# Unnormalised softmax, two products per value block, and fractional shares of background work in an attention stage on one Trainium2 core

## The chip, the cores and the metric

The kernel runs on one core of one Trainium2 chip. The core has a matrix engine (PE, with a weight-load track PEld), a vector engine (DVE), an activation engine (ACT), a general engine (POOL, GpSimd) and a queue engine (SP) that mostly starts DMAs. The engines run their own instruction streams in order and wait for each other through semaphores. The metric is the device time of one execution in microseconds; lower is better. All times below are microseconds unless marked ns.

## The reference, cut to what matters

One layer of a streaming encoder: a half-step feed-forward block, one combined projection, sparse attention beside a convolution module, a gated merge with an output projection, and a second half-step feed-forward block. There are 1088 rows (1024 prompt rows and 64 sample rows). The part that the change touches:

```python
z = u @ w_in                       # [q | k | v | q_idx | k_idx | w_idx | conv in | branch gates]
# attention: 8 heads of 64 in 2 groups; each query keeps its top-k admissible keys
logits = einsum('bqcgd,bqncd->bqcgn', qg, kg) * HEAD_DIM ** -0.5
p = softmax(where(valid, logits, -inf))
o = einsum('bqcgn,bqncd->bqcgd', p, vg)
# convolution module
conv_out = silu(layernorm(dc)) @ conv_w_out
# merge
g_a, g_c = split(sigmoid(gate + b_gate), 2)
merged = g_a * (attn @ attn_w_out) + g_c * conv_out
h = h + merged @ w_out
```

All arithmetic is in 32 bits. A product with full precision is made of three matrix products of reduced operands: each operand is split into a high and a low part, and high x high, high x low and low x high are added up in PSUM (`mm3`).

## The kernel before

Activations lie with channels on partitions and rows in the free dimension. Rows are cut into three chunks of 364, 362 and 362 columns (`CHUNKS`). The stages in order: first feed-forward block, combined projection with convolution and indexer, search for the top-k thresholds on DVE, attention, output projection, second feed-forward block. Weights come in by DMA on SP (`wload`: `raw`), are split by ACT (`whi`) and POOL (`wlo`), and the buffers are three deep.

**The gates.** `gates` computes the 16 gate tiles, each three steps (one for each chunk) of 24 matmuls, and ACT's tanh and a DMA (started on ACT's queue) that writes them to DRAM (`d_g`). The first `GPRE` = 8 tiles run ahead of attention, while DVE is still busy with the search; the others are background work of the attention stage.

**Attention.** Queries are taken in nine tiles (`ATILES`): eight of 128 rows with 128 (i + 1) keys, and tile 8 with 64 rows and 192 keys. The order is `TORD` = 8, 5, 6, 7, 4, 3, 2, 1, 0. Each tile has four pairs of heads. For a pair, `soft` computes the logits (two matmuls `lg` for each head and half, L999 and L1000), DVE adds the mask and takes the maximum (L1002), then small DVE instructions join the halves and scale (L1008, L1010), ACT takes the exponential with its sum (L1012), DVE the reciprocal (L1014), and POOL (first head) and DVE (second head) multiply the weights `pr` by it (L1016). `turn` takes a slot of up to two key blocks, transposes four pieces of `pr` by PE (`pt`, L1026) and splits them by ACT and DVE (`ph`, `pl`). `values` adds up the values with `mm3`, so three matmuls of 256 columns for a block with a stationary operand 64 columns wide (`vt`: high or low part); the result `pv` has 64 partitions. After the last block ACT copies it (`oh`) and a DMA writes it to DRAM (`d_at`).

Logits run `AHEAD` = 2 pairs ahead, values `LAG` = 2 slots behind.

**Background work.** `fill` is called once for each slot (84 slots in all) and runs so many steps of `background` as `FILL` has for the tile. Background is one chain: the remaining gates; `norm` of chunk 2 (layer norm of the convolution's output, read from `d_dc`); `conv_out` of chunks 2, 1, 0, each with the `norm` of the chunk that follows; `merge` of chunk 2, which loads the attention's output (`ar`), splits it (`ah`, `al`) and, for each of eight output tiles, loads a gate (`ga`) and a convolution tile (`mpt`), makes 12 matmuls and combines them on DVE (L1162, L1163); `wout` of chunk 2; `merge` of chunk 1. A `merge` starts only after `ready` has found the attention tiles of its chunk done. After attention come `wout` of chunk 1, `merge` of chunk 0, `wout` of chunk 0.

**PSUM.** There are eight banks. Before attention, four belong to `ps4` (used by the gates) and four to `lgi` (indexer, DVE part of the convolution, search). At the start of attention these are closed and pools are opened in this order: `lgp` (three banks, logits), `psf` (two, background), `psa` (two, transposes), `pvp` (one, values). The order of the instructions on each engine is made when the program is built, from the order in which the code issues them, priorities, and a model of when each could run.

## Time and profile before

| what | us |
|---|---|
| median of three runs | 2391.95 (2390.51 to 2393.91) |
| the profiled execution | 2394.14 |
| its span, first to last instruction | 2392.3 |
| PE busy in the span | 2300.3 |
| DVE, POOL, ACT busy in the span | 1658.8, 1407.1, 1146.8 |
| attention stage, from the first logits to the last values | 1157.5 to 1536 |

Times inside the span count from its first instruction. PE is nearly always marked busy. Matmuls overlap, so the duration of one (289 ns for 272 columns) is more than its share of PE's time; what one costs in a full stream is the distance from its start to the next one's start.

### The profile page before, as it was taken

How to read it: one execution, taken by the hardware profiler on the slowest of the kernel's cores; microseconds unless marked ns; L12 is line 12 of the kernel's file. 1: busy time of each engine (PE TensorE's matmuls, PEld its weight loads, DVE VectorE, ACT ScalarE, POOL GpSimd, SP SyncE). 2: the span in 40 equal slices, each digit the busy share in tenths (PEclk: the TensorE clock that was granted, in tenths of full speed). 3: DMA queues.
4: the chain of work that ended last, by engine and by line, in shares of the span. 5: the costliest groups of instructions: out<-in, count | busy, mean ns of one | idle time of the engine just before them, and what ended most of it. 6: DMA issues, size and time to landing. Idle time of an engine off the chain costs nothing.

```text
span 2392.3 us, 43870 instructions
## 1 busy us (share of the span) xinstructions
PE 2300.3 (96%) x16762; PEld 2272.8 (95%) x16762; DVE 1658.8 (69%) x3606; ACT 1146.8 (48%) x2189; POOL 1407.1 (59%) x861
## 2 busy tenths in 40 slices
PE   5999999999999999999899899899999999999997
PEld 5999999999999999999898889899999999999997
DVE  7666678677567387579535897468766678776676
ACT  5433445444335546875644565345433445334343
POOL 4555556555556686889853455457455565445554
PEclk9999999999999999999999999999999999999999
DMA  4232332332223443333322446753232332332223
GB/s 166 89 104 91 98 98 90 125 107 98 89 90 121 143 138 121 91 120 120 106 78 96 125 135 204 254 167 113 80 100 92 107 103 72 108 108 97 89 98 117
DMA packets 130116, 271.90 MB, mean 114 GB/s; under 512 B 18032, under 2 KB 77296, under 8 KB 129904
## 3 DMA queue, kind: packets, MB, share of 16 engines
q1 hardware_dynamic: 114688, 253.48, 32.6%
q10 hardware_dynamic: 15216, 15.60, 2.0%
q8 instruction: 132, 2.16, 0.4%
q14 instruction: 80, 0.66, 0.1%
HBM read 230.34 MB, written 38.75 MB: 112 GB/s over the span
## 4 chain that ended last, share of the span: by engine, by line
PE 76%; DVE 9%; DMA 6%; POOL 4%; issue 2%; ACT 2%; SPq 0%; ACTq 0%; DVEq 0%; POOLq 0%
PE ps L154 24%; PE ps L156 24%; PE ps L155 24%; POOL ac L695 3%; DMA ga<-d_g 1%; PE pt L1026 1%; PE lgi L806 1%; PE lgi L807 1%; DMA d_h<-hr 1%; DVE ga L1163 1%; DMA raw<-wf 1%; DMA raw<-d_k 1%; PE ps L184 1%; DMA d_mp<-gc 1%; DVE t L229 1%
## 5 line engine op out<-in xcount | busy, mean ns | idle before, releaser
L137 POOL TENSOR_TENSOR wlo<-raw,whi 128x1024 fp32r<-128x1024 f32 (+1 forms) x187 | 435.9, 2335 | 352.3 <-ACT whi L136 343.5
L154 PE MATMUL ps<-x,wp 128*128 128x272 f32 x1760 | 508.4, 290 | 10.9 <-DVE spare L302 9.3
L155 PE MATMUL ps<-x,wp 128*128 128x272 f32 x1760 | 506.8, 289 | 0.0
L156 PE MATMUL ps<-x,wp 128*128 128x272 f32 x1760 | 506.1, 291 | 0.8 <-DVE wp L171 0.4
L154 PE MATMUL ps<-x,whi 128*128 128x272 f32 (+2 forms) x1544 | 483.1, 313 | 9.3 <-ACT x L170 4.3
L156 PE MATMUL ps<-x,wlo 128*128 128x272 f32 (+2 forms) x1544 | 481.2, 312 | 0.0
L155 PE MATMUL ps<-x,whi 128*128 128x272 f32 (+2 forms) x1334 | 412.7, 309 | 0.0
L154 PE MATMUL ps<-gh,whi 128*128 128x272 f32 x1408 | 399.8, 289 | 6.8 <-DVE spare L302 5.0
L155 PE MATMUL ps<-gl,whi 128*128 128x272 f32 x1408 | 404.7, 289 | 0.0
L156 PE MATMUL ps<-gh,wlo 128*128 128x272 f32 x1408 | 403.5, 288 | 0.0
L171 POOL TENSOR_TENSOR wlo<-raw,whi 128x1024 fp32r<-128x1024 f32 x88 | 220.4, 2505 | 261.6 <-ACT whi L170 253.2
L154 PEld LDWEIGHTS ps<-x,wp 128*128 128x128 f32 x1760 | 332.9, 189 | 11.7 <-ACT wp L170 11.6
L155 PEld LDWEIGHTS ps<-x,wp 128*128 128x128 f32 x1760 | 333.3, 189 | 0.0
L156 PEld LDWEIGHTS ps<-x,wp 128*128 128x128 f32 x1760 | 330.7, 189 | 2.5 <-DVE wp L171 2.1
L171 POOL TENSOR_TENSOR wp<-s,wp 128x512 fp32r<-128x512 f32 x176 | 256.6, 1458 | 97.2 <-ACT wp L170 97.2
L154 PEld LDWEIGHTS ps<-x,whi 128*128 128x128 f32 x1544 | 293.2, 190 | 11.3 <-ACT x L170 4.7
L136 ACT ACTIVATE whi<-raw 128x1024 fp32r<-128x1024 f32 (+1 forms) x187 | 190.6, 1020 | 218.1 <-PE ps L155 116.8
L156 PEld LDWEIGHTS ps<-x,wlo 128*128 128x128 f32 x1544 | 293.3, 190 | 0.9
L442 DVE SCALAR_TENSOR_TENSOR h<-ps,h 128x272 f32<-128x272 f32 x384 | 164.3, 438 | 184.9 <-PE ps L156 184.4
L695 POOL TENSOR_TENSOR ac<-ac,pd 128x559 f32<-128x559 f32 x180 | 260.9, 1449 | 35.2 <-ACT pd L694 11.8
L154 PEld LDWEIGHTS ps<-gh,whi 128*128 128x128 f32 x1408 | 262.9, 189 | 8.3 <-DVE spare L302 5.7
L156 PEld LDWEIGHTS ps<-gh,wlo 128*128 128x128 f32 x1408 | 265.7, 189 | 0.0
(238 smaller groups left out, 4782.0 us busy)
## 6 DMA issues: line engine op xcount, KB each, us to landing
raw<-wf SPq DMA_DIRECT2D x334, 512.0 KB, 3.3
raw<-wf SPq DMA_DIRECT2D x32, 384.0 KB, 3.1
d_g<-sg ACTq DMA_DIRECT2D x32, 181.0 KB, 1.9
d_h<-h SPq DMA_DIRECT2D x2, 2176.0 KB, 10.4
y<-t SPq DMA_DIRECT2D x32, 136.0 KB, 1.8
raw<-d_q SPq DMA_DIRECT2D x32, 128.0 KB, 2.7
raw<-d_qi SPq DMA_DIRECT2D x24, 128.0 KB, 3.0
d_g<-sg ACTq DMA_DIRECT2D x16, 182.0 KB, 1.9
```

What stands on the lines that cost most here:

```text
L136: nc.scalar.activation(hi[:, :n], raw[:, :n], AF.Copy)
L137: self.weng.tensor_tensor(lo[:, :n], raw[:, :n], hi[:, :n], op=ALU.subtract)
L154: t.matmul(out, wh, xh, start=first, stop=False)
L155: t.matmul(out, wh, xl, start=False, stop=False)
L156: t.matmul(out, wl, xh, start=False, stop=last)
L171: (eng or nc.vector).tensor_tensor(lo, x, hi, op=ALU.subtract)
L184: self.nc.tensor.matmul(ps[:, b * P:(b + 1) * P], x[:, t0:t0 + P], self.ones, start=i == 0, stop=i == len(tiles) - 1)
L229: self.nc.vector.scalar_tensor_tensor(x, h[:, k, t0:t0 + w], self.par[:, q:q + 1], r, op0=ALU.mult, op1=ALU.mult)
L442: nc.vector.scalar_tensor_tensor(x, p, 0.5, x, op0=ALU.mult, op1=ALU.add)
L695: nc.gpsimd.tensor_tensor(ac, ac, pd, op=ALU.add)
L806: nc.tensor.matmul(o, qt[:, hd, :], kih[:, ks:ks + pw], start=True, stop=False)
L807: nc.tensor.matmul(o, qt[:, hd, :], kil[:, ks:ks + pw], start=False, stop=True)
```

## The change

- `soft`: the logits get scale -0.125 in the same DVE instruction as the mask, and the minimum in place of the maximum, carried on from one half to the next. So the instructions L1008 and L1010 are gone, and the exponential of a head starts as soon as that head is done. The multiplication with the reciprocal (L1016) is gone; the reciprocals of a tile's eight heads are collected in `rs`.
- `values`: the value tile `vt` is laid out so that high and low part stand side by side as one stationary operand of 128 columns. Two matmuls for a block (with `ph` and with `pl`) in place of three; the result has 128 partitions: the high part's result on the lower 64, the low part's on the upper. Once for each tile the reciprocals are transposed by PE, copied by ACT and written to DRAM (`d_rs`).
- `merge`: loads both halves for each head and the reciprocals (spread over 64 partitions), adds the halves, multiplies, and then splits as before.
- `GPRE` is 9 rather than 8. `FILL` has fractions: they are added up, and a step is run for each whole.
- `lgp` is opened after `psf` and `psa`. `oh` has four buffers rather than two.

```diff
-GPRE = 8
+GPRE = 9
-FILL = {7: 1, 6: 1, 8: 2, 5: 1, 4: 1, 3: 2, 2: 2, 1: 2, 0: 2}
+FILL = {8: 1, 5: 0.6, 6: 0.6, 7: 0.8, 4: 1.2, 3: 2, 2: 2, 1: 3, 0: 3}
...
-            d_at = dram.tile([512, T], F32, name="d_at")
+            d_at = dram.tile([8, P, T], F32, name="d_at")
+            d_rs = dram.tile([8, T], F32, name="d_rs")
...
-            vt = ak.tile([P, 2, 10, P], F32R, name="vt")
+            vt = ak.tile([P, 10, 2, 2, 64], F32R, name="vt")
...
-            lgp = self.pool(at_es, "lg", NLG, space=PS)
             psf = self.pool(at_es, "psf", 7 - NLG - NPT, space=PS)
             psa = self.pool(at_es, "psa", NPT, space=PS)
+            lgp = self.pool(at_es, "lg", NLG, space=PS)
...
-                        nc.vector.tensor_tensor_reduce(p[:, b * pw:(b + 1) * pw], o, bias[:rows, bo:bo + pw],
-                                                       1.0, -3e38, op0=ALU.add, op1=ALU.max,
-                                                       accum_out=mb[:rows, hh, b:b + 1])
-                        if (hh, b) == (1, nb - 1):
-                            mm = mb[:rows, :, 0]
-                            if nb == 2:
-                                nc.vector.tensor_tensor(mx[:rows, :], mm, mb[:rows, :, 1], op=ALU.max)
-                                mm = mx[:rows, :]
-                            nc.vector.tensor_scalar(mx[:rows, :], mm, -0.125, None, op0=ALU.mult)
-                            for e in range(2):
-                                nc.scalar.activation(u.pr[e], u.pr[e], AF.Exp, bias=mx[:rows, e:e + 1],
-                                                     scale=0.125, accum_out=sm[:rows, e:e + 1])
-                            nc.vector.reciprocal(sm[:rows, :], sm[:rows, :])
-                            for e in range(2):
-                                {'P': nc.gpsimd, 'V': nc.vector}[SC[e]].tensor_scalar(u.pr[e], u.pr[e], sm[:rows, e:e + 1], None, op0=ALU.mult)
+                        nc.vector.tensor_tensor_reduce(p[:, b * pw:(b + 1) * pw], o, bias[:rows, bo:bo + pw], -0.125,
+                                                       mn[:rows, hh, 0:1] if b else 3e38,
+                                                       op0=ALU.add, op1=ALU.min, accum_out=mn[:rows, hh, b:b + 1])
+                        if b == nb - 1:
+                            nc.scalar.activation(p, p, AF.Exp, bias=mn[:rows, hh, b:b + 1], scale=-1.0,
+                                                 accum_out=sm[:rows, hh:hh + 1])
+                            if hh:
+                                nc.vector.reciprocal(rs[:, u.h0:u.h0 + 2], sm[:rows, :])
...
-                    vh = vt[:kn, 0, vb, 64 * u.g:64 * u.g + 64]
-                    vl = vt[:kn, 1, vb, 64 * u.g:64 * u.g + 64]
                     c = slice(n * s_, n * s_ + n)
-                    self.mm3(u.pv, vh, vl, ph[:kn, c], pl[:kn, c], first and s_ == 0, last and s_ == len(slot) - 1)
+                    vv = vt[:kn, vb, u.g, :, :].rearrange("p a d -> p (a d)")
+                    nc.tensor.matmul(u.pv, vv, ph[:kn, c], start=first and s_ == 0, stop=False)
+                    nc.tensor.matmul(u.pv, vv, pl[:kn, c], start=False, stop=last and s_ == len(slot) - 1)
                 if last:
                     if u.h0 == 6:
                         done.add(u.i)
-                    oh = ap_.tile([64, 256], F32, name="oh", tag="oh", bufs=2)[:, :n]
+                        pt = psa.tile([P, 512], F32, name="pt", tag="pt")[:8, :u.rows]
+                        nc.tensor.transpose(pt, rss[u.i][:u.rows], ident[:u.rows, :u.rows])
+                        rt = ap_.tile([8, P], F32, name="rt8", tag="rt8", bufs=2)[:, :u.rows]
+                        nc.scalar.activation(rt, pt, AF.Copy)
+                        nc.scalar.dma_start(d_rs[:, u.t0:u.t0 + u.rows], rt)
+                    oh = ap_.tile([P, 256], F32, name="oh", tag="oh", bufs=4)[:, :n]
...
+                rs = mp_.tile([P, 4, WMAX], F32, name="rw", tag="rw")[:, :, :w]
+                for e in range(2):
+                    nc.sync.dma_start(rs[64 * e:64 * e + 64],
+                                      d_rs.rearrange("(k e) c -> e k c", e=2)[e:e + 1, :, c0:c0 + w].to_broadcast([64, 4, w]))
                 for k in range(4):
-                    ar = mp_.tile([P, WMAX], F32, name="ar", tag="ar", bufs=2)[:, :w]
-                    nc.sync.dma_start(ar, d_at[k * P:(k + 1) * P, c0:c0 + w])
-                    self.split(ah[:, k, :], al[:, k, :], ar, nc.gpsimd if k % 2 else nc.vector)
+                    ar = mp_.tile([P, 2, WMAX], F32, name="ar", tag="ar", bufs=2)[:, :, :w]
+                    for e in range(2):
+                        nc.sync.dma_start(ar[64 * e:64 * e + 64],
+                                          d_at[2 * k + e, :, c0:c0 + w].rearrange("(a d) c -> d a c", a=2))
+                    eng = nc.gpsimd if k % 2 else nc.vector
+                    eng.tensor_tensor(ar[:, 0, :], ar[:, 0, :], ar[:, 1, :], op=ALU.add)
+                    eng.tensor_tensor(ar[:, 0, :], ar[:, 0, :], rs[:, k, :], op=ALU.mult)
+                    self.split(ah[:, k, :], al[:, k, :], ar[:, 0, :], eng)
...
+            due = [0]
             def fill(units, n):
-                u = units[n]
-                for _ in range(FILL[u.i]):
+                due[0] += FILL[units[n].i]
+                while due[0] >= 1:
+                    due[0] -= 1
                     next(bg, None)
```

More of the change, by code (lines that the diff above doesn't have):

```diff
@@ L35 @@
 AHEAD, LAG = 2, 2
-SC = 'PV'
 RB = 2
@@ L938, in run @@
             nc.sync.dma_start(raw[:SMP, 9, :], d_v[:SMP, 9, :])
-            self.split(vt[:, 0, 0:9, :], vt[:, 1, 0:9, :], raw[:, 0:9, :])
-            self.split(vt[:SMP, 0, 9, :], vt[:SMP, 1, 9, :], raw[:SMP, 9, :])
+            for g in range(2):
+                for r, b in ((P, slice(0, 9)), (SMP, slice(9, 10))):
+                    self.split(vt[:r, b, g, 0, :], vt[:r, b, g, 1, :], raw[:r, b, 64 * g:64 * g + 64])
             AORD = TORD
@@ L986, in soft @@
                 pw = L // nb
-                mb = ap_.tile([P, 8, 2], F32, name="mb", tag="mb", bufs=AHEAD + 1)[:, 0:2, :]
-                mx = ap_.tile([P, 2], F32, name="mx", tag="mx", bufs=AHEAD + 1)
+                mn = ap_.tile([P, 2, 2], F32, name="mn", tag="mn", bufs=AHEAD + 1)
                 sm = ap_.tile([P, 2], F32, name="sm", tag="sm", bufs=AHEAD + 1)
+                if u.h0 == 0:
+                    rss[u.i] = ap_.tile([P, 8], F32, name="rs", tag="rs", bufs=2)
+                rs = rss[u.i][:rows]
                 u.pr = []
@@ L1036, in turn @@
                 return ph, pl
+            rss = {}
             def values(u, slot, ph, pl):
@@ L1041, in values @@
                 if first:
-                    u.pv = pvp.tile([P, 512], F32, name="pv", tag="pv")[:64, 0:n]
+                    u.pv = pvp.tile([P, 512], F32, name="pv", tag="pv")[:, 0:n]
                 for s_, (vb, kk, kn) in enumerate(slot):
-                    vh = vt[:kn, 0, vb, 64 * u.g:64 * u.g + 64]
-                    vl = vt[:kn, 1, vb, 64 * u.g:64 * u.g + 64]
                     c = slice(n * s_, n * s_ + n)
-                    self.mm3(u.pv, vh, vl, ph[:kn, c], pl[:kn, c], first and s_ == 0, last and s_ == len(slot) - 1)
+                    vv = vt[:kn, vb, u.g, :, :].rearrange("p a d -> p (a d)")
+                    nc.tensor.matmul(u.pv, vv, ph[:kn, c], start=first and s_ == 0, stop=False)
+                    nc.tensor.matmul(u.pv, vv, pl[:kn, c], start=False, stop=last and s_ == len(slot) - 1)
                 if last:
@@ L1050, in values @@
                         done.add(u.i)
-                    oh = ap_.tile([64, 256], F32, name="oh", tag="oh", bufs=2)[:, :n]
+                        pt = psa.tile([P, 512], F32, name="pt", tag="pt")[:8, :u.rows]
[4 more added lines that the diff above has]
+                    oh = ap_.tile([P, 256], F32, name="oh", tag="oh", bufs=4)[:, :n]
                     nc.scalar.activation(oh, u.pv, AF.Copy)
                     nc.scalar.dma_start(
-                        d_at[64 * u.h0:64 * u.h0 + 128, u.t0:u.t0 + u.rows].rearrange("(h d) c -> d h c", d=64),
-                        oh.rearrange("d (h c) -> d h c", h=2))
+                        d_at[u.h0:u.h0 + 2, :, u.t0:u.t0 + u.rows].rearrange("h p c -> p h c"),
+                        oh.rearrange("p (h c) -> p h c", h=2))
             def attention(units, fill):
```

## The prediction

> **What bounds the kernel now.** I read the page's totals first, then a table of stretches around attention, then PE's waits, then the order of time where PE waits longest.
>
> ```profile
> span 2392.3 us, 43870 instructions
> PE 2300.3 (96%) x16762; PEld 2272.8 (95%) x16762; DVE 1658.8 (69%) x3606; ACT 1146.8 (48%) x2189; POOL 1407.1 (59%) x861
> ```
>
> PE is busy for 96% of the span, so work taken from PE can show. But an average doesn't say that it does so in attention. The change touches only the time from about 1147 to 1605, which the next view cuts (columns: length, then busy time and instructions of PE, PEld, DVE, ACT, POOL, then granted clock, DMA share, GB/s).
>
> ```profile
> 1147.00:1160.00 13.00, 6.12 (x33) 5.82 (x32) 4.74 (x9) 7.78 (x12) 12.61 (x8) 0.72 0.29 99
> 1160.00:1290.00 130.00, 130.00 (x835) 126.45 (x835) 51.05 (x140) 69.23 (x134) 72.93 (x43) 0.99 0.27 84
> 1290.00:1430.00 140.00, 125.81 (x876) 116.84 (x874) 126.34 (x325) 87.81 (x185) 68.16 (x35) 0.98 0.43 129
> 1430.00:1513.00 83.00, 79.36 (x516) 77.79 (x514) 50.75 (x114) 38.26 (x83) 48.44 (x27) 1.00 0.62 194
> 1513.00:1540.00 27.00, 18.96 (x106) 17.62 (x105) 22.18 (x33) 11.55 (x26) 12.45 (x7) 0.91 0.75 241
> ```
>
> Four different limits stand side by side. Before 1160 PE has nothing it may start. From 1160 to 1290 (gates beside attention) PE is the limit: no idle time, and DVE at 39%. From 1290 to 1430 (layer norms and convolution output beside attention) DVE is busy for 126.34 of 140, 90%, and PE sits idle for 14.2: here DVE and the chains through it share the limit. From 1513 (last merge of the stage) PE has 8.0 idle again. What PE waits for in the whole stage:
>
> ```profile
> PE ps L154 <- DVE ga L1162: 7.8, 5, 3.8
> PE lg L999 <- ACT sg L952: 6.9, 1, 6.9
> PE pv L154 <- ACT oh L1052: 6.7, 4, 3.5
> ```
>
> The first is the merge's loop at the end, the second is one gap at the start, the third is the single `pv` bank waiting for its copy.
>
> **The products with the values.** Two matmuls replace three. Their number comes from the view of the tile `pv`, their price from starts in a full stream: values, then a gate's matmuls; below, logits that have the shape that the new products get (256 columns against a stationary operand of 128x128).
>
> ```profile
> L154 PE MATMUL pv<-ph,vt x152: 222/280/476, 1179.4 to 1535.6; 128*64 128x256 f32 x144, 128*64 128x128 f32 x4, 64*64 64x128 f32 x4
> ```
> ```profile
> 1244.76 0.28 PE L154 MATMUL pv<-ph,vt 128*64 128x256 f32 x1
> 1244.88 0.28 PE L155 MATMUL pv<-pl,vt 128*64 128x256 f32 x1
> ...
> 1245.46 0.33 PE L154 MATMUL ps<-x,whi 128*128 128x362 f32 x1
> 1245.63 0.33 PE L155 MATMUL ps<-x,whi 128*128 128x362 f32 x1
> ...
> 1459.60 0.28 PE L1000 MATMUL lg<-kl,qt 128*128 128x256 f32 x1
> 1459.72 0.28 PE L999 MATMUL lg<-kh,qt 128*128 128x256 f32 x1
> ```
>
> Six value matmuls lie between 1244.76 and 1245.46: 0.117 each, though each is marked 0.28. The logits with full-width weights are 0.12 apart too, so twice the weight columns should cost nothing. Of 152 blocks each loses one matmul: 144 x 0.117 = 16.8, and eight with half the columns at about 0.06 (an estimate from those), 0.5. **Sum: -17.3.** Bounds: 0 where PE isn't the limit, and below nothing if wide loads aren't hidden (a rival).
>
> One rule speaks against this. The Trainium skill, "TensorE: Matmul & The Clock Gate", section "LDWEIGHTS (loading the stationary operand)", gives a load's time as its columns divided by 1.2 GHz, which makes 53 ns for 64 columns and 107 ns for 128. By an estimate from that page, with loads not hidden at all, 456 products at 53 + 109 ns become 304 at 107 + 109 ns, and only 8 of the 17.3 are saved. The logits rows show them hidden; I keep -17.3.
>
> **The gap at the start, the order of the PSUM pools and the ninth gate tile.**
>
> ```profile
> 1150.29 0.32 PE L156 MATMUL ps<-x,wlo 128*128 128x362 f32 x1
> 1157.50 0.42 PE L999 MATMUL lg<-kh,qt 128*64 128x192 f32 x1 [6.88 <-ACT sg L952]
> ...
> 1158.52 0.56 PE L154 MATMUL ps<-x,whi 128*128 128x364 f32 x1
> 1158.87 0.51 PE L155 MATMUL ps<-x,whi 128*128 128x364 f32 x1
> 1159.18 0.51 PE L156 MATMUL ps<-x,wlo 128*128 128x364 f32 x1
> ```
> ```profile
> 1156.90 0.54 ACT L952 ACTIVATE sg<-ps,hb 128x362 f32<-128x362 f32 x1
> 1145.97 3.50 POOL L137 TENSOR_TENSOR wlo<-raw,whi 128x1024 fp32r<-128x1024 f32 x1 [2.25 <-ACT whi L136]
> 1159.75 0.35 DVE L1002 CUSTOM_DVE_ANT_0 pr<-lg,bias 64x192 f32<-64x192 f32 x1 [8.13 <-DMA d_g<-sg]
> ```
>
> The last gate matmul starts at 1150.29; the first logits wait until 1157.50 for ACT's evacuation of the last gate (1156.90, late behind the convolution on ACT). I read this as banks: `lgp`, opened first, gets banks of the gates' pool. Behind that one wait stands the ninth gate tile at 1158.52, although its weights were ready at 1149.47 (1145.97 + 3.50). Afterwards the logits get banks of `lgi`, and the ninth tile runs in the old pool ahead of attention, so PE can go on at 1150.4. The tile itself (72 matmuls 0.167 apart, 12) is moved, not saved. The gap is worth 6.9, and slow matmuls after it (0.31 apart at 1158.87 rather than 0.17, some nine of them, 1.3) make 8.2. What is late next: `pr` waits for the DMA of the last gate, one tile later now; the tenth gate tile (12 of PE) covers that wait, but needs `psf` banks that ACT has to free. **I take -7**, bounds -8.2 and 0; nearer to the first, since ready work stands behind the wait.
>
> **The stage from 1290 to 1430.** What goes there, for L1016 (columns after the length: DVE, POOL) and for the tile `mx` (DVE, ACT; DVE's part is L1008 and L1010), and how many value products lie there:
>
> ```profile
> 1290.00:1430.00 140.00, 8.97 (x15) 35.71 (x16) 0.98 0.43 129
> ```
> ```profile
> 1290.00:1430.00 140.00, 7.67 (x25) 28.65 (x64) 0.98 0.43 129
> ```
> ```profile
> 1290.00:1430.00 140.00, 43.60 (x261) 31.82 (x259) 5.52 (x15) 0.98 0.43 129
> ```
>
> DVE loses 8.97 + 7.67 = 16.6 and would be busy for 109.7, 78% of the stage; POOL loses 35.7 of 68.2. PE's own saving there, 261 / 3 x 0.117 = 10.2, is already in the -17.3. The 14.2 idle and a stretch at a low clock are what may come on top:
>
> ```profile
> 1420.00:1430.00 10.00, 10.00 (x53) 9.80 (x52) 8.74 (x24) 5.91 (x16) 5.03 (x4) 0.71 0.15 47
> 1430.00:1440.00 10.00, 10.00 (x71) 9.94 (x70) 7.81 (x17) 5.66 (x12) 6.04 (x4) 1.00 0.56 177
> ```
>
> 53 rather than 71 matmuls: 18 / 71 x 10 = 2.5. Together 16.7. The exponential no longer waits for the other head, nor the transposes for L1016, and four `oh` buffers loosen the `pv` wait. But the norms are serial chains of DMA, DVE and PE, which stay. **I take half, -8**, bounds -16.7 and +10.2 (PE's saving turns into idle time).
>
> **What is added.** PE: nine small transposes of the reciprocals, a few of them stalling nothing; at 0.1 each **+1**. They take a `psa` bank; behind them stand the next slots' transposes. ACT: nine copies and nine DMA issues; ACT is at 48%. The merge's prologue:
>
> ```profile
> L171 POOL TENSOR_TENSOR al<-ar,ah x6: 970/1099/1258, 1354.7 to 1559.7; 128x362 fp32r<-128x362 f32 x4, 128x364 fp32r<-128x364 f32 x2
> ```
> ```profile
> DMA to landing us min/median/max: 2.2/3.5/7.3
> ```
>
> There are two buffers for four pieces, so two rounds: landing 3.5, ACT copy some 0.5, POOL 1.1, that is 5.1 a round. Two more POOL instructions make it 7.3: +4.4 for each chunk, plus six more DMA issues on SP (0.3 to 0.4 each), behind which the weight loads stand. Attention covers it for chunk 2, and `wout` of chunk 1 (eight tiles of 24 matmuls, 32) for chunk 0. Chunk 1's stands open: **+4**, bounds 0 and 13. The twelve new instructions on DVE may also meet this:
>
> ```profile
> 1523.54 2.78 DVE L1163 SCALAR_TENSOR_TENSOR ga<-mpt,ga 128x362 f32<-128x362 f32 x1
> ```
> ```profile
> 1523.52 2.41 POOL L137 TENSOR_TENSOR wlo<-raw,whi 128x1024 fp32r<-128x1024 f32 x1 [3.58 <-ACT whi L136]
> ```
>
> A DVE instruction with two SBUF inputs stretched to 2.78 while POOL split a weight (0.54 without). That is 12 x 2.2 = 27 of DVE time at worst, most of it off the path. The Trainium skill, "SBUF — State Buffer", section "SBUF: two separate sides", says that DVE with two SBUF inputs and a POOL instruction that reads SBUF exclude each other for the whole instruction; by it the added sums pay while the removed L1016 frees POOL. The two rows agree with it.
>
> **The other mix of background work.** Tiles 8, 5, 6, 7 have 4, 12, 16, 16 slots. Up to the end of tile 7 the old table gives 8 + 12 + 16 + 16 = 52 steps, the new one 4 + 7.2 + 9.6 + 12.8 = 33.6, and three were moved ahead: 15 steps fewer. The work is the same; what changes is how much attention is left beside the merges. Old order: `merge` of chunk 1 already runs almost bare. New: it starts in tile 1 at three steps a slot. I take **0**, bounds -8.0 (the idle time after 1513) and, as a rival, much more.
>
> **Sum.** -17.3 - 7 - 8 + 1 + 4 = -27.3. The profiled execution took 2394.1, hence 2366.8; the median of the runs is 2.2 lower, so about 2365 to 2367: I say **2366**.
>
> **Rivals.** One more row, value products between 1430 and 1513, is for the third:
>
> ```profile
> 1430.00:1513.00 83.00, 10.33 (x66) 8.10 (x66) 2.84 (x8) 1.00 0.62 194
> ```
>
> - *DVE and the chains still pace 1290 to 1430.* PE's 10.2 there becomes idle and nothing else closes: -17.3 + 10.2 - 7 + 1 + 4 = -9.1, some 2384. For it: 90% DVE and serial norms. Against: 16.6 of DVE gone from that very stage. Chance 0.20.
> - *All gaps close*: -17.3 - 8.2 - 16.7 - 8.0 + 1 = -49.2, some 2344. For it: each named wait is touched. Against: the last is a loop of loads that stays. Chance 0.10.
> - *Slower: attention runs out before the background.* The 15 deferred steps leave both merges bare. The bare merge after 1513 took 26 for eight tiles of 12 matmuls at 0.167 (16): 10 lost, 7 more than what chunk 2's merge loses now with 3.6 idle between 1430 and 1513. Both prologues (2 x 14.6) stand open in place of the +4, and three cold restarts cost some 5: -17.3 - 7 - 8 + 1 + 7 + 29 + 5 = +9.7, some 2402. It decides if the last attention transposes come before chunk 2's first merge matmul. Against: the rows of `pv` put 66 / 3 = 22 blocks of attention into that stretch, and the new order has more left.
> - *The change doesn't save PE time*: the wide weight load isn't hidden. PEld marks 0.19 for 128 columns; 304 x 0.19 against 456 x 0.117 is +4, in all -6, some 2386. Against: the logits rows. Chance 0.05.
>
> **How the numbers follow.** Forecast (2356 to 2377) 0.55, the rivals 0.20, 0.10, 0.09 and 0.05, the rest 0.01. The range 2348 to 2388 holds the forecast, the first and the last rival and part of the second. About 0.2% is what a measurement of this kernel can tell, here 4.8. Faster 0.84, same 0.07, slower 0.09.
>
> **What would show it.** Right: `pv` products 0.117 apart, 304 of them; no wait of logits for `sg`, gates running through 1150; PE idle in the norm stage under 10, DVE under 85%; `ar` loads with a longer prologue before chunk 1's merge. Wrong: `pv` about 0.19 apart; the start gap back under another name (the `psf` bank, or `pr`); PE idle of 20 or more around the merges because the attention rows have ended.

## The result, and the profile after

The changed kernel takes **2416.75 us** (median of 4 runs, 2410.99 to 2420.96) beside 2391.23 of the kernel before (4 runs, 2384.43 to 2393.91): a ratio of 1.0109, with a 95% interval from 1.0079 to 1.0140. The forecast was 2366 and its range ended at 2388. The sign was wrong.

The profiled execution took 2420.96. Its totals, from the page of the kernel after:

```profile
span 2419.2 us, 43520 instructions
PE 2296.9 (95%) x16619; PEld 2268.3 (94%) x16619; DVE 1621.4 (67%) x3532; ACT 1149.3 (48%) x2200; POOL 1360.2 (56%) x837
```

The change took away what it promised: net 143 records of PE, 74 of DVE, 24 of POOL. Yet PE is *busy* for only 3.4 less, and the span is 27 longer. The table of stretches says where (length, then busy time and count of PE, PEld, DVE, ACT, POOL, then granted clock, DMA share, GB/s):

```profile
1147.00:1160.00 13.00, 12.71 (x77) 12.42 (x76) 0.00 (x0) 7.30 (x11) 9.29 (x7) 1.00 0.36 129
1160.00:1290.00 130.00, 121.81 (x779) 117.33 (x778) 51.84 (x143) 80.99 (x160) 55.29 (x34) 0.97 0.27 87
1290.00:1430.00 140.00, 126.60 (x852) 118.77 (x850) 112.25 (x291) 90.32 (x207) 32.83 (x22) 0.95 0.52 150
1430.00:1513.00 83.00, 57.34 (x291) 54.69 (x292) 37.40 (x68) 24.27 (x53) 31.08 (x16) 0.84 0.69 208
```

From 1147 to 1160 PE now runs through, as forecast. From 1290 to 1430 DVE has fallen from 90% to 80%, as forecast, but PE is as idle as before (13.4 beside 14.2) and its clock is lower (0.95 beside 0.98). From 1430 to 1513 it goes wrong: PE starts 291 matmuls there rather than 516, idles for 25.7 and is granted 0.84.

One row each gives the whole account. It goes from 1140, where both kernels stand alike, to the start of the last matmul of `wout` of chunk 0 on `xh`; what follows takes 765 in both. The kernel before, then the kernel after:

```profile
1140.00:1627.60 487.60, 452.59 (x2901) 435.78 (x2901) 317.48 (x751) 258.50 (x519) 272.33 (x150) 0.97 0.46 145
```
```profile
1140.00:1654.70 514.70, 450.54 (x2764) 433.12 (x2763) 282.24 (x663) 261.01 (x531) 220.52 (x129) 0.94 0.49 151
```

Idle time of PE is length less busy time: 35.0 before, 64.2 after. The granted clock stands at 1.00 or at 0.50 in these traces. What it cost is half of the time that PE was busy at 0.50; idle time at the low clock is counted as idle already. The sums over the stretches at 0.50, before and after:

```profile
sum 27.31, PE 19.90 PEld 19.64 DVE 15.83 ACT 14.52 POOL 16.35; mean PE 4.98 PEld 4.91 DVE 3.96 ACT 3.63 POOL 4.09
```
```profile
sum 61.43, PE 42.73 PEld 41.14 DVE 28.70 ACT 19.86 POOL 18.86; mean PE 4.75 PEld 4.57 DVE 3.19 ACT 2.21 POOL 2.10
```

That makes 10.0 before and 21.4 after. What is left is PE's work at full clock: 442.6 before, **429.2** after. So the matmuls did become some 13 cheaper, where the forecast's terms for PE were 17.3 less 1, and 29.2 more idle time and 11.4 more of low clock took it back and 27 on top. An engine that reads "95% busy" had not been the limit in most of the stages from which the work was taken.

### The profile page after: what moved, and what is told of

Its sections match the earlier page's. It is cut to its first block, busy times and chain, and to the rows that moved or that the text cites. A ratio compares the mean times of both kernels' runs of the same rounds, so it can differ in the third digit from the quotient of the medians.

```text
span 2419.2 us, 43520 instructions
## 1 busy us (share of the span) xinstructions
PE 2296.9 (95%) x16619; PEld 2268.3 (94%) x16619; DVE 1621.4 (67%) x3532; ACT 1149.3 (48%) x2200; POOL 1360.2 (56%) x837
## 4 chain that ended last, share of the span: by engine, by line
PE 77%; DVE 8%; DMA 7%; POOL 4%; issue 2%; ACT 2%; SPq 0%; DVEq 0%; ACTq 0%; POOLq 0%
PE ps L153 24%; PE ps L155 24%; PE ps L154 24%; POOL ac L695 4%; DMA ga<-d_g 1%; PE pt L1022 1%; PE lgi L806 1%; PE lgi L807 1%; DMA rw<-d_rs 1%; DMA d_h<-hr 1%; DMA ci<-d_c 1%; DMA d_mp<-gc 1%; DMA gc<-d_g 1%; DVE ps L329 0%; DVE pl L170 0%
## 5 line engine op out<-in xcount | busy, mean ns | idle before, releaser
L153 PE MATMUL ps<-x,wp 128*128 128x272 f32 x1760 | 508.2, 290 | 11.4 <-DVE spare L301 9.3
L695 POOL TENSOR_TENSOR ac<-ac,pd 128x559 f32<-128x559 f32 x180 | 266.5, 1481 | 39.3 <-ACT pd L694 13.9
L441 DVE SCALAR_TENSOR_TENSOR h<-ps,h 128x272 f32<-128x272 f32 x384 | 164.4, 438 | 184.7 <-PE ps L155 184.2
```

What stands on the lines that cost most here:

```text
L153: t.matmul(out, wh, xh, start=first, stop=False)
L441: nc.vector.scalar_tensor_tensor(x, p, 0.5, x, op0=ALU.mult, op1=ALU.add)
L695: nc.gpsimd.tensor_tensor(ac, ac, pd, op=ALU.add)
```

## The theories

- **A**: the new table runs attention out ahead of the background, so the merges run bare. This is the forecast's "slower" rival.
- **B** and **E**: the merge itself has become dearer (two loads for each piece, reciprocals, an added sum and a product).
- **C**: the ninth gate tile delays the start.
- **D**: the loads of `h` for the second feed-forward block collide with the merge. They are issued on ACT's queue as soon as attention's SBUF is free.
- **P**, formed after the first runs: the chain of background work (gates, norms, `conv_out`, merge, `wout`) sets the end, and attention only fills it.

The deciding point of the "slower" rival came true. The last transposes of attention against the first matmul of chunk 2's merge, from the views of the tiles `pt` and `ah` of the kernel after:

```profile
L1022 PE MATMUL pt<-ident,pr x304: 216/272/421, 1180.1 to 1453.1; 128*128 128x128 f32 x144, 64*128 64x64 f32 x4, 64*64 64x64 f32 x4
```
```profile
L153 PE MATMUL ps<-ah,whi x96: 322/328/641, 1466.7 to 1618.2; 128*128 128x362 f32 x64, 128*128 128x364 f32 x32
```

The order of time beside them shows D at work. ACT's queue issues two loads of `h` (1448 KB each) as attention ends, and the next issue, attention's own last output, blocks the queue for 7.66:

```profile
1464.51 0.59 ACTq L1266 DMA_DIRECT2D h<-d_h  x1
1465.14 0.67 ACTq L1266 DMA_DIRECT2D h<-d_h  x1
1465.91 7.66 ACTq L1056 DMA_DIRECT2D d_at<-oh  x1
```
```profile
1470.00:1480.00 10.00, 4.84 (x30) 4.54 (x28) 5.78 (x5) 2.90 (x4) 4.93 (x2) 0.96 1.05 380
1480.00:1490.00 10.00, 5.84 (x21) 5.87 (x22) 3.85 (x9) 0.95 (x2) 0.00 (x0) 0.52 0.65 224
```

The DMA engines are full at 380 GB/s, PE gets through 51 matmuls in 20 us, and in the second slice its clock is 0.52. In the kernel before the same loads were issued from 1538.0 on, and `wout` of chunk 1 started at 1540.0: its merge was through.

## The experiments

### Which half of the change costs: the mix or the arithmetic

`old_mix` is the changed kernel with the old table and eight gate tiles; `old_fill` and `gpre8` each put one of the two back. `before_newmix` is the kernel before with the new table and nine tiles.

```diff
# old_mix = both lines; old_fill = the second alone; gpre8 = the first alone
-GPRE = 9
+GPRE = 8
-FILL = {8: 1, 5: 0.6, 6: 0.6, 7: 0.8, 4: 1.2, 3: 2, 2: 2, 1: 3, 0: 3}
+FILL = {7: 1, 6: 1, 8: 2, 5: 1, 4: 1, 3: 2, 2: 2, 1: 2, 0: 2}
```

> The changed kernel with the old table of background steps and eight gate tiles ahead; the softmax, the two-product values, the merge and the order of the pools stay new. Theory A (the new mix runs attention out ahead of the background, and the merges then run bare): the saving in arithmetic shows, 2365 to 2380, attention's last values no earlier than about 1500. Theory B (the heavier merge, with reciprocals and twice the attention output to load, costs): 2400 or more, with idle PE around the merges as in the changed kernel. Theory C (the ninth gate tile delays attention's start): as theory A, since GPRE is 8 here.

> The kernel before with only the new table of fractions and nine gate tiles ahead; softmax, values, merge and pools are the old ones. Theory A: slower than before by 20 to 45 (2412 to 2437), attention over 40 to 70 us ahead of the end of the background. Theory B: about 2392, since the merge is the old one. Theory C: 2395 to 2405, by a longer wait at the start alone.

> The changed kernel with the old table of steps but nine gate tiles ahead. Theory A: as with both undone, 2365 to 2380. Theory B: 2400 or more. Theory C: 2410 or more, since the ninth tile is still ahead.

> The changed kernel with eight gate tiles ahead but the new table of fractions. Theory A: as slow as the changed kernel or slower (2412 to 2430), since three more steps lie behind the same table. Theory B: 2400 or more. Theory C: 2375 to 2395.

| kernel | median | ratio to before, 95% |
|---|---|---|
| old_mix | 2413.91 | 1.0093 (1.0076 to 1.0110) |
| before_newmix | 2412.92 | 1.0098 (1.0081 to 1.0115) |
| old_fill | 2408.09 | 1.0079 (1.0060 to 1.0097) |
| gpre8 | 2429.82 | 1.0161 (1.0144 to 1.0178) |

Each half alone costs some 22, and both together (the change) 25: they don't add. So the mix, which the forecast held at 0, costs 22 on the old arithmetic, within the range that A gave for it, but only 3 on the new; and the arithmetic, which it held at -27, costs 22 without the mix, which A can't explain. For the changed kernel C fell: with nine tiles it is 6 (old table) or 13 (new table) faster than with eight. On the kernel before, the ninth tile alone costs 5 (`before_gpre9`, below), within C's range.

### The loads of h, and the reciprocals in the merge

The hold: each load of `h` waits for a word that DVE copies from the last result of chunk 1's merge, and chunk 1 is loaded first. `old_mix_norw` leaves the load of `rw` and the product with it out of the merge.

```diff
-            for c0, w in CHUNKS[::-1]:
+            for c0, w in (CHUNKS[1], CHUNKS[2], CHUNKS[0]):
+                nc.vector.tensor_copy(h[:, 7, c0:c0 + 1], M[1][1][:, 7, 0:1])
                 nc.scalar.dma_start(h[:, :, c0:c0 + w], d_h[:, :, c0:c0 + w])
...
# old_mix_norw, old_htied_norw
-                rs = mp_.tile([P, 4, WMAX], F32, name="rw", tag="rw")[:, :, :w]
...
-                    eng.tensor_tensor(ar[:, 0, :], ar[:, 0, :], rs[:, k, :], op=ALU.mult)
```

> The changed kernel with the old mix, and the three loads of the residual h (1.4 MB each, started on ACT's queue) held back until chunk 1's merge has written its last tile, chunk 1 first. Theory D (these loads start as soon as attention's memory is free; where attention ends before the merge, they block ACT's queue and fill the DMA engines while the merge still needs both): 2392 to 2402, against 2414 without the hold; no wait of ACT of over 5 us between 1530 and 1550, the granted clock back above 0.9 there. Theory E (the merge's own heavier loads cost, wherever h is loaded): 2408 to 2418, unchanged.

> The changed kernel with the same hold on the loads of h. Theory D: 2395 to 2408, the 9 us wait in chunk 2's merge gone. Theory E, and theory A (attention has run out, the merges are bare): 2412 to 2420.

> The kernel before with the same hold. There the loads already start when the merge is all but done. Theory D: 2386 to 2396, no change, or some us slower where the first output product waits for h. Theory E: the same.

> The changed kernel with the old mix, leaving out the division by the softmax sums: the merge neither loads the reciprocals (two transfers of 362 KB for each chunk) nor multiplies by them. Theory E: 2395 to 2405, since this load is the longest of the merge's (6.3 us) and half of its new instructions go. Theory D: 2408 to 2414, since the loads of h still meet the merge.

> The change with the old table and eight tiles ahead (2413.9), with both remedies: the loads of h held until the merge of chunk 1 is done, and the load of the reciprocals and the multiplication by them left out of the merge (so the division by the softmax sums is left out). If the collision with h and the merge's own loads are two costs that add up: 2390 to 2395, all of the 22 accounted for. If they are one and the same wait (whichever goes, the other one takes it): 2400 to 2406. If the forecast's savings were still there behind them: 2375 or below.

| kernel | median | ratio to before, 95% |
|---|---|---|
| old_mix_htied | 2404.11 | 1.0054 (1.0037 to 1.0071) |
| after_htied | 2411.86 | 1.0083 (1.0066 to 1.0100) |
| before_htied | 2392.81 | 1.0005 (0.9996 to 1.0015) |
| old_mix_norw | 2403.09 | 1.0047 (1.0030 to 1.0064) |
| old_htied_norw | 2391.63 | 0.9990 (0.9978 to 1.0002) |

The hold gives 10 to the change with the old table, 5 to the change, and nothing to the kernel before: the collision is new. It accounts for less than D promised: the held kernels were to come to 2392 to 2402 and 2395 to 2408. `before_newmix` wasn't run with the hold; there too ACT's queue stands for 6.45 behind these loads, so part of the mix's 22 may be D's. Leaving out the reciprocals gives 11 (the four runs lie between 2393.95 and 2405.39, wider apart than the others), and both together 22. With the old table the two costs add up to the whole loss of the arithmetic. The price of the reciprocals can be seen in the view of the tile `rw` of the kernel after: POOL (11.7 in two waits) and DVE (10.9 in three) wait for the load, and it lands late.

```profile
  DMA rw<-d_rs: 22.6, 5
...
  POOL ar L1162: 11.7, 2
  DVE ar L1162: 10.9, 3
...
DMA to landing us min/median/max: 5.8/6.5/7.2
```

Whether the load or the product behind it is the dearer part wasn't taken apart. How the collision looks with the old table: from `old_mix`, stretches and order of time where chunk 1's merge runs.

```profile
1530.00:1540.00 10.00, 4.20 (x26) 3.99 (x25) 3.57 (x7) 2.35 (x4) 2.69 (x2) 0.96 0.85 215
1540.00:1550.00 10.00, 5.01 (x15) 4.54 (x16) 2.67 (x6) 0.51 (x1) 0.00 (x0) 0.50 1.05 319
1550.00:1560.00 10.00, 2.97 (x10) 2.50 (x9) 4.02 (x4) 3.18 (x6) 5.41 (x4) 0.67 1.06 356
```
```profile
1539.57 6.49 ACTq L1056 DMA_DIRECT2D d_at<-oh  x1
1546.10 1.26 ACTq L1266 DMA_DIRECT2D h<-d_h  x1
1547.41 0.51 ACT L169 ACTIVATE xh<-ga 128x362 fp32r<-128x362 f32 x1 [12.19 <-issue]
```

ACT stood idle for 12.19. The three DMA issues on its queue from 1538.24 on (0.53, 6.49 and 1.26) fill 8.3 of that, and the split of `ga` runs right behind them; for the rest the trace shows no cause ("issue": no other wait is seen). PE started 51 matmuls in 30 us.

But when the two costs are gone, the kernel is where it was before, not 27 below. The savings themselves are missing.

### Are the value products worth anything?

`old_mix_third` is `old_mix` with a third product for each block; the low part of the weights is counted twice.

```diff
                     nc.tensor.matmul(u.pv, vv, ph[:kn, c], start=first and s_ == 0, stop=False)
+                    nc.tensor.matmul(u.pv, vv, pl[:kn, c], start=False, stop=False)
                     nc.tensor.matmul(u.pv, vv, pl[:kn, c], start=False, stop=last and s_ == len(slot) - 1)
```

> The change with the old table and eight gate tiles ahead (2413.9), with a third value product for each block put back: the low part of the softmax weights is counted twice, so 456 value products of 256 columns instead of 304; nothing else is touched. My forecast's term (each product is worth 0.117 where PE is the limit): 17 slower, some 2431. Theory P (attention's products are filler beside a background chain that has its own pace): 0 to 6 slower, 2414 to 2420; or even faster, if the longer attention covers more of the merge.

It takes **2409.14** (1.0065, 1.0043 to 1.0086): not slower than `old_mix` at all, for 152 matmuls more. The total alone proves less than it seems to, as the lengths by stretch show. They go from 1140 to the first layer norm's load (`lx`), from there to the last matmul of `conv_out` (`ch`), and from there to the last `wout` (`xh`); `pv_only` comes further down.

| kernel | to `lx` | to the last `ch` | to the last `xh` |
|---|---|---|---|
| before | 148.8 | 157.7 | 181.1 |
| before_newmix | 166.8 | 154.6 | 183.1 |
| after | 164.6 | 159.0 | 191.1 |
| old_mix | 146.6 | 156.4 | 206.8 |
| old_mix_third | 149.6 | 155.5 | 196.3 |
| pv_only | 144.1 | 175.1 | 193.8 |

In the first stretch, with 36 products more (4.2 by their price), the kernel is 3.0 longer, which is no more than kernels with `old_mix`'s code up to there differ (142.2 to 148.4). In the last, with 17 more, the kernel is 10.5 shorter: attention ends later, the loads of `h` go out from 1548.0 rather than 1534.3, and less of the collision is left. The pair wasn't run with the hold, so the total mixes this gain with the price of the products. What decides is the norm stage between them. From the first layer norm's load to the last matmul of `conv_out`, the whole stretch and then the value products in it; `old_mix`, then `old_mix_third`:

```profile
1286.60:1443.00 156.40, 140.09 (x907) 130.43 (x906) 126.70 (x309) 98.40 (x208) 43.34 (x26) 0.93 0.54 154
```
```profile
1286.60:1443.00 156.40, 38.22 (x194) 28.40 (x194) 6.43 (x17) 0.93 0.54 154
```
```profile
1289.60:1445.10 155.50, 143.75 (x1010) 135.42 (x1009) 127.68 (x310) 99.69 (x209) 43.14 (x26) 0.99 0.51 154
```
```profile
1289.60:1445.10 155.50, 49.28 (x293) 39.78 (x293) 6.41 (x17) 0.99 0.51 154
```

Within 1.3 us the same work on DVE, ACT and POOL, 99 value products more, and the stage is 0.9 *shorter*. At 0.117 each the 99 are 11.6. In their absence PE idles 4.6 more, and it is busy at half clock for 18.0 rather than 3.2, which costs 7.4 more. The same stage takes 152 to 156 in the five kernels that have `old_mix`'s code up to there, so it is the 99 products' 11.6 that is missing, and in this stage they are free. Slices of 10 us show what PE runs beside; two of the kernel before, then two of `old_mix`:

```profile
1370.00:1380.00 10.00, 7.05 (x47) 6.29 (x46) 10.00 (x24) 5.89 (x13) 5.21 (x4) 1.00 0.40 115
...
1410.00:1420.00 10.00, 6.47 (x47) 5.95 (x45) 10.00 (x20) 7.85 (x18) 4.62 (x2) 0.94 0.35 101
```

```profile
1360.00:1370.00 10.00, 7.74 (x51) 6.69 (x50) 10.00 (x17) 7.03 (x15) 3.71 (x2) 0.93 0.49 145
...
1410.00:1420.00 10.00, 6.94 (x37) 5.96 (x36) 10.00 (x20) 7.19 (x18) 3.96 (x3) 0.82 0.39 121
```

DVE, the third column of times after the length, is full (10.00) in the layer norms while PE idles. An average of 80 or 90% over the stage hides it. In the kernel before, the four slices with DVE at 9.94 or more hold 9.7 of PE's 14.2 idle. In `old_mix` three such slices hold 7.7 of 16.3; another 3.3 lie in a slice with DVE at 5.35, so there DVE accounts for about half, and the rest isn't traced to one engine.

### The chain earlier

If P holds, more steps early should help. `fast_htied` is `after_htied` with an early table (65 steps up to the end of tile 7, rather than 34 in the change and 52 before); `before_fast` is the kernel before with that table and nine tiles; `before_gpre9` has nine tiles alone.

```diff
+FILL = {8: 2, 5: 1.25, 6: 1.25, 7: 1.375, 4: 1, 3: 1, 2: 1, 1: 3, 0: 3}
```

> The changed kernel, with the loads of h held until the merge of chunk 1 is done, and the background steps spread the other way: FILL {8: 2, 5: 1.25, 6: 1.25, 7: 1.375, 4: 1, 3: 1, 2: 1, 1: 3, 0: 3}, so about 65 steps up to the end of tile 7 instead of 34 (before: 52). Theory P (the background chain is the path that sets the end, attention only fills it: the norm and convolution stage took 154 to 160 us in all kernels but one, whatever ran beside it): the layer norm of chunk 2 starts near 1275 instead of 1300, everything behind it moves with it, and the time falls 15 to 40 below the same kernel with the late mix (2411.9), to 2372 to 2397. Theory A alone (only the cover of the merges counts, so attention should last as long as possible) and theory E (only the merge's own loads count): no more than 10 lower, 2402 or above, as the end of the chain would still be bare.

> The kernel before, its arithmetic untouched, with nine gate tiles ahead and the same early fractions as fast_htied (about 65 steps up to the end of tile 7, before 52). Theory P: the chain starts some 12 earlier and the time falls below the kernel before, to 2365 to 2388. If instead the old table already holds the balance, the two products and the other edits being what costs: 2388 to 2400. If attention beside the chain is what sets the pace from 1290 to 1430 (my forecast's reading): no gain, 2390 or above, as the chain only starts sooner and then runs beside the same attention.

> The kernel before with nine gate tiles ahead of attention instead of eight, nothing else. Theory P: three steps fewer in front of the norm and convolution chain, so it starts about 6 earlier for a start of attention that is 12 later and no longer stalls: 3 to 8 faster, 2384 to 2389. Theory C (the ninth tile delays the start and its wait comes back): 0 to 8 slower. With the change and the old table the same step gave -6 (2413.9 to 2408.1).

| kernel | median | ratio to before, 95% |
|---|---|---|
| fast_htied | 2404.01 | 1.0048 (1.0034 to 1.0062) |
| before_fast | 2394.07 | 1.0001 (0.9992 to 1.0011) |
| before_gpre9 | 2399.22 | 1.0021 (1.0008 to 1.0035) |

P promised 15 to 40 for the first, and times below the kernel before for the others: it got 8, nothing, and a loss of 5. Why, from the first and last starts in the views of tiles:

| start of | before | before_fast | before_newmix | after_htied | fast_htied |
|---|---|---|---|---|---|
| first layer norm's load (`lx`) | 1288.8 | 1280.9 | 1306.8 | 1299.6 | 1275.7 |
| last `conv_out` (`ch`) | 1446.5 | 1445.3 | 1461.4 | 1459.6 | 1435.4 |
| last value product (`pv`) | 1535.6 | 1540.3 | 1479.4 | 1460.1 | 1534.1 |
| last `wout` (`xh`) | 1627.6 | 1631.2 | 1644.5 | 1643.1 | 1631.5 |

With the old arithmetic the chain started 8 earlier and gave it back within the norm stage, which went from 157.7 to 164.4. With the new arithmetic the chain kept its lead of 24 up to the end of `conv_out` and lost half of it behind that, since attention now still had to be worked off beside the merges. So P is half right. A late chain is paid for in full (`before_newmix`: 18 late at the norms, 17 late at the end). An early one meets the next limit. This doesn't clear A. Of the 12.0 that PE idles more in `before_newmix`, 11.0 lie behind the last `conv_out`, where attention is gone from 1479.4 on and the merges run bare. Deferred steps show as a late chain to one who counts from the start, and as bare merges to one who counts PE's idle time; no run here separates the two. The ninth tile's loss of 5 came by neither P's path nor C's: in `before_gpre9` the norms start 7.4 earlier, but their stage takes 168.7 rather than 157.7.

### The two halves of the arithmetic alone

`pv_only` is the kernel before with the wide products, both halves through DRAM and their sum in the merge, and four `oh` buffers, with the old softmax. `soft_only` has only the minimum carried on and the earlier exponential, and keeps the multiplication. `soft_order` opens `lgp` last as well. `pv_only_htied` adds the hold. `old_htied_ar4` is `old_mix_htied` with four buffers of `ar`.

```diff
# soft_order
-            lgp = self.pool(at_es, "lg", NLG, space=PS)
             psf = self.pool(at_es, "psf", 7 - NLG - NPT, space=PS)
             psa = self.pool(at_es, "psa", NPT, space=PS)
+            lgp = self.pool(at_es, "lg", NLG, space=PS)
...
# old_htied_ar4
-                    ar = mp_.tile([P, 2, WMAX], F32, name="ar", tag="ar", bufs=2)[:, :, :w]
+                    ar = mp_.tile([P, 2, WMAX], F32, name="ar", tag="ar", bufs=4)[:, :, :w]
```

> The kernel before with the two value products for a block alone: wide value tile, both halves to DRAM, halves added in the merge, four buffers of oh; the softmax with its multiplication by the reciprocals, the order of the PSUM pools, the table and the eight tiles ahead stay as before. My forecast's step: -17 for the products and +4 for the prologue, 2379. Theory P with E (products are filler, the doubled loads and the added sums stand in the merge, which is on the path): 2395 to 2412. No effect at all would be 2393.

> The kernel before with only the first part of the softmax edit: scale and minimum in the mask's instruction, the small joining instructions gone, the exponential of each head as soon as its logits are done; the multiplication by the reciprocals and everything else stays. My forecast's term for the norm stage was -8, of which DVE's 7.7 of joining instructions and the earlier exponential are this part: some 2387 to 2390. Theory P in its strict form (the norm chain's pace doesn't depend on attention's instructions): 2390 to 2396. Where DVE is full in the layer norm's slices and that sets the pace: 2385 to 2390.

> soft_only with the PSUM pools opened in the changed order (psf and psa ahead of lgp), eight gate tiles ahead. My forecast's term for the start is -7 with the ninth tile; with eight tiles the first logits should come some 6 earlier (1151 rather than 1157, as in the change with the old table), and if that is passed on, the time is 3 to 7 below soft_only. Theory P: the gates in front of the norm chain are PE work that gains only what PE's idle time was there; 0 to 4 below soft_only.

> The kernel before with the two value products alone (2421.9) and the loads of h held until the merge of chunk 1 is done. If its loss is the collision with h, as for a part of the change with the old table: 10 to 15 lower, 2407 to 2412. If it is the norm stage that stretched (the trace of the product edit alone has 117.6 of 140 busy from 1290 to 1430, at a clock of 0.91): no more than 4 lower, 2418 or above.

> The change with the old table, eight tiles ahead and the loads of h held back (2404.1), and four buffers of ar instead of two, so that the four pieces of a merge are loaded at once. If the merge's loads cost by their two rounds (the forecast's reading, 4.4 to 7.3 for each chunk): 2392 to 2399. If they cost by their volume and by the reciprocals' load in front of them: 2402 to 2406.

| kernel | median | ratio to before, 95% |
|---|---|---|
| pv_only | 2421.89 | 1.0110 (1.0091 to 1.0130) |
| soft_only | 2395.21 | 1.0007 (0.9996 to 1.0019) |
| soft_order | 2396.98 | 1.0013 (1.0001 to 1.0024) |
| pv_only_htied | 2411.74 | 1.0085 (1.0056 to 1.0114) |
| old_htied_ar4 | 2404.04 | 1.0051 (1.0032 to 1.0071) |

The part of the softmax edit that `soft_only` has gains nothing on the old arithmetic, and the pools' order nothing on top, although the first logits start at 1150.0 rather than 1156.8. The products alone are the worst kernel but one, above every range that was on record for them, though not in the first stretch, where PE is full: with 36 products fewer, 4.2 by their price, it takes 144.1 and 144.7 (`pv_only_htied`), against 148.8 and 146.4 in the kernel before and `before_htied`. The collision with `h` is 10 of their 29. Most of the rest is in the norm stage, whose last `conv_out` matmul starts at 1459.2 rather than 1446.5; from `pv_only`:

```profile
1290.00:1430.00 140.00, 117.62 (x742) 107.00 (x741) 126.64 (x308) 82.38 (x173) 62.55 (x34) 0.91 0.46 131
```

DVE is as busy as before (126.6 of 140), PE idles 22.4 instead of 14.2 and is granted 0.91. Why this stage gets longer than with three products, rather than staying as long, isn't settled. `old_mix` has the same products beside the new softmax, and there the stage takes 156.4 rather than 175.1, so DVE's relief may be worth more beside two products than `soft_only` shows. But `gpre8`, with every edit of the arithmetic, takes 172.0 for it: the builder orders the instructions anew for each kernel, and that order wasn't held fixed. Four buffers of `ar` change nothing, so the merge's loads don't cost by their rounds.

The account of the first section for the other kernels (same start, each to its own last start on `xh`):

| kernel | length | PE idle | lost by the clock | PE's work at full clock |
|---|---|---|---|---|
| before | 487.6 | 35.0 | 10.0 | 442.6 |
| soft_only | 490.2 | 40.7 | 6.2 | 443.3 |
| before_newmix | 504.5 | 47.0 | 13.2 | 444.2 |
| old_mix_third | 501.4 | 44.9 | 8.1 | 448.4 |
| after | 514.7 | 64.2 | 21.4 | 429.2 |
| old_mix | 509.8 | 58.8 | 21.9 | 429.1 |
| fast_htied | 491.5 | 46.6 | 16.4 | 428.5 |
| old_htied_norw | 486.3 | 41.2 | 13.8 | 431.3 |

Four kernels with three products need 443 to 448 at full clock, four with two need 429 to 431. The work is always saved, and the length of the whole stretch doesn't follow it.

No kernel of these beats the one before.

## Why the prediction was wrong, by its steps

- **"Two matmuls replace three ... Sum: -17.3."** The price was right, the place wrong. From the order of time of the kernel after, the products are 0.12 apart with the wide operand, and the loads are hidden:

```profile
1245.47 0.28 PE L1044 MATMUL pv<-ph,vt 128*128 128x256 f32 x1
1245.59 0.28 PE L1045 MATMUL pv<-pl,vt 128*128 128x256 f32 x1
1245.71 0.28 PE L1044 MATMUL pv<-ph,vt 128*128 128x256 f32 x1
1245.83 0.28 PE L1045 MATMUL pv<-pl,vt 128*128 128x256 f32 x1
```

  So the rival "the change doesn't save PE time" fell. But the forecast's own bound, "0 where PE isn't the limit", was the value to take for the norm stage: it had seen DVE at 90% there and still counted 10.2 of the 17.3 in full. Putting the third product back cost nothing in that stage. Only where PE is full, ahead of the norms, is a saving to be seen (2 to 5 with the products alone, 4.2 by their price).
- **"The stage from 1290 to 1430 ... I take half, -8."** The part of it in `soft_only` (the joining instructions and the earlier exponential) gave 0; taking the multiplication out wasn't run alone. With both and three products (`old_mix_third`) the norm stage is 2.2 shorter than before. Its length stayed at 152 to 161 in 15 of the 20 kernels, and was 164 to 175 in the other five. Of the 16.6 taken from DVE, 11.5 lie outside the four slices of 10 us in which DVE of the kernel before is full, and 5.1 in them. A high average was read as one limit, where there are bursts and gaps.
- **"I take -7" for the start.** The wait of the logits is gone, and it came back under another name, as the forecast had feared: the tenth gate tile waits for a `psf` bank until ACT has worked through its gates. The row, from the order of time of the kernel after:

```profile
1172.60 0.67 PE L153 MATMUL ps<-x,whi 128*128 128x364 f32 x1 [8.20 <-ACT sg L953]
```

  6.9 had gone, 8.20 came (5.53 in `old_mix`, with eight tiles). The order of the pools was not the limit: ACT evacuates the gates between convolution instructions that wait for POOL. In the middle of the wait POOL, the fifth column of times after the length, is busy for 4.76 of 5, ACT for 2.73 and PE not at all:

```profile
1165.00:1170.00 5.00, 0.00 (x0) 0.00 (x0) 0.00 (x0) 2.73 (x4) 4.76 (x4) 0.86 0.39 137
```

- **"+4" for the prologues, bounds 0 and 13.** The mechanism (more to load ahead of a merge) was right and the term too small: the reciprocals' part alone, which the term did not hold, measures 11 to 12.5 with the old table. The rounds of `ar` weren't the reason.
- **"I take 0" for the mix.** It costs 22 on the kernel before, the largest error of a single term there (of the 22, the ninth gate tile alone gives 5), though only 3 beside the changed arithmetic. The forecast counted 15 steps fewer and asked only for the cover of the merges. In `before_newmix` that cover is missing, with 11.0 more of PE's idle time behind the last `conv_out`. And the chain itself is late: the norms start 16 to 18 later in the kernels with the new table, and nothing behind them makes it good.
- **Not seen at all:** that attention's end frees the memory into which `h` is loaded, so that an earlier end sends two of its loads (three with the old table) of 1.4 MB each into a merge. It costs 5 in the change and 10 with the old table.
- The rival **"attention runs out before the background"** named the right deciding point, and its 2402 came within 15, but partly by luck: it carried along three savings that the total doesn't show, and the 41 that it put on bare merges (7, 29 and 5, the first 6.4 by its own numbers) is more than the last stretch gained, 19.8 of idle time and 5 by the clock. Its chance of 0.09 rested on the value products between 1430 and 1513 in the old trace; the new fractions shift just these.

## What to carry to other kernels

Before a saving on a busy engine is counted, ask in each stage which engine is full in slices as short as the chains in it, and count the saving only where that is the same engine; elsewhere it can become idle time. Where filler runs beside a chain, count the steps of the chain by time and not only the cover that is left: late steps are paid in full. When a phase is made to end earlier, look up what its end releases.

## What the runs showed of the hardware

**Idle time can be paid twice.** PE's clock falls after gaps that are short and not even whole. From `old_mix`, slices of 2.5 us around the second full DVE slice above:

```profile
1410.00:1412.50 2.50, 2.50 (x19) 2.47 (x18) 2.50 (x7) 2.50 (x6) 0.00 (x0) 1.00 0.43 127
1412.50:1415.00 2.50, 1.63 (x11) 1.07 (x9) 2.50 (x3) 2.50 (x7) 2.15 (x1) 1.00 0.00 0
1415.00:1417.50 2.50, 0.74 (x2) 0.36 (x2) 2.50 (x5) 0.07 (x2) 1.50 (x2) 0.78 0.37 123
1417.50:1420.00 2.50, 2.07 (x7) 2.07 (x8) 2.50 (x9) 2.12 (x6) 0.30 (x1) 0.50 0.76 235
1420.00:1422.50 2.50, 2.50 (x12) 2.42 (x12) 1.76 (x5) 0.71 (x2) 0.86 (x1) 0.50 0.18 60
1422.50:1425.00 2.50, 2.50 (x17) 2.50 (x17) 2.08 (x6) 1.26 (x3) 0.00 (x0) 0.86 0.00 0
```

PE was idle for 2.6 of the 5 us of the second and third rows, in waits of which the trace's longest is 1.45. By the 0.78 of the third row and the 0.86 of the last, the clock was at 0.50 from about 1416.4 to 1423.2: a full slice then starts 12 matmuls, where the first row has 19. Every stretch at 0.50 that is in the two sums of the first section lasts 3.4, 6.8 or 10.2. The Trainium skill, "TensorE: Matmul & The Clock Gate", section "Part 1: The HAM clock gate (the "warmup" mystery)", puts the fall to half after an idle window of some 3.4 us. The half speed agrees; the gap that was enough here is shorter and broken up, and the measurement decides. This is why the account above has a column for the clock: in the change it took back 11 of the 13 by which PE's work fell.

**A DMA issue on ACT can block ACT.** Behind two loads of `h` (1448 KB each) the next issue on the same queue stood for 7.66 in the kernel after, 6.49 in `old_mix` and 5.10 in the kernel before. In the first two ACT started nothing until it was through. An ordinary issue there takes 0.3 to 0.7.
